# Down projection of a hybrid streaming layer: the next chunk's weight steps at fixed places over the chunk

## The chip, the cores and the metric

The kernel runs on one core of one Trainium2 chip. The metric is the time of one execution on the device in microseconds (us), the median of several runs; lower is better. Profiles show one execution, with the engines named PE (TensorE matmuls), PEld (TensorE weight loads), DVE (VectorE), ACT (ScalarE), POOL (GpSimd) and SP (SyncE, which issues DMAs).

## The reference, cut to what matters

One layer of a hybrid encoder is computed for 2048 prompt rows and 128 sample rows (17 tiles of 128 rows), in float32. The change touches only the last product of the feed-forward part:

```python
h = rmsnorm(x, norm_ffn_pre)
f = (jax.nn.silu(h @ w_gate) * (h @ w_up)) @ w_down     # w_down: 2816 x 1024
x = x + rmsnorm(f, norm_ffn_post)
```

## The kernel before, in words

**Stages.** The program runs the input projection and the two mixers, the output projection, gate and up, and last the down projection with the final norm. The down projection is the last stage; all before it stays as it is.

**How the down product is tiled.** The 22 blocks of 128 rows of `w_down` are cut into five chunks, `FCHUNKS`: four of 4 blocks and a last one of 6. Within a chunk two blocks make a 2 x 2 arrangement of quarters (b11, b12, b21, b22, each 128 x 512), and there are c = 2 such arrangements (q = 0, 1) in a chunk, c = 3 in the last. The product is done by a seven-product scheme in the manner of Strassen: step i = 0 to 6 multiplies one combination of activation rows by one combination of the quarters. Rows are taken in pairs of tiles: there are eight pairs (`pairs`, numbered 0 to 7 here) and one single tile. In each chunk the first two pairs run interleaved (the duo), then comes the single tile (four products), then pairs 2 to 7, one after the other; in the last chunk the single tile comes ahead of pair 7.

**Precision.** Every operand is split into a rounded part and the rest: a cast on ACT makes the first, a subtraction makes the second. Each product (`product`, L1567) is therefore 3 x c matmuls of 128 x 128 by 128 x 512, which read weights `dw` (or `sA` to `sD`, which serve as slots of the same ring) and activations `as`: 6 matmuls in a chunk with c = 2, 9 in the last.

**Activations.** `load_parts` (L1560) loads `ar` with SP's queue. `split` (L1551) casts on ACT (L1554) and subtracts (L1557): on DVE for i = 0 and 3 (in the last chunk i = 0 alone), on POOL for the rest. There are six `as` buffers (`NDA`), so the cast of a product waits until the product six before it has been done.

**Sums.** The result of a step goes from one of eight PSUM banks into `acc` in SBUF: by an addition on DVE (`acc_add`, L1534), in chunk 0 partly by a copy on ACT (L1614). A pair uses four banks; the bank of step 0 is used again by step 4, that of 1 by 5 and so on, so DVE has the time of three products to add a step's result before PE needs its bank. In the last chunk the finished rows are normed and stored as well (`finish`, L1577).

**The preparation of weights** is what the change moves. `down_chunk` (L1212) is a generator; each step of it either loads a q (two DMAs of `dr` from `w_dn` on SP's queue, L1220, into four `dr` buffers) or makes one part (i, q): for i = 1, 2, 3, 5 a subtraction of quarters on DVE (L1227 to L1233), then a cast on ACT (L1244), then the rest (L1246), every third on DVE and the others on POOL. A chunk with c = 2 has 2 loads and 14 parts. Parts go into a ring of `NDW` = 21 slots, so with a chunk's 14 parts in place there is room for seven of the next, and the other seven need slots that the current chunk's last pair gives free, two after each of its products. `prep_step(n)` runs n steps. It is called while a product lacks its weights (L1570), after each product of the last pair with n = c (L1666), and after pairs 2 to 6 with a share of `spare` = 9 (L1720). A step that finds the generator exhausted moves to the next chunk's generator and does nothing else.

**What sets the order.** A scheduler in the build writes the order of each engine's queue, and may set an instruction ahead of its place in the code where it finds its inputs ready. `tc.issue_after(ins)` holds the instructions of its block behind `ins` in the queue of the engine of `ins`. The queues of the engines then run in that order.

Of the kernel before, what the change touches and what calls it, by code (L numbers as in the profile page):

```python
# [9 lines left out]
F32 = mybir.dt.float32  # L10
# [3 lines left out]
ALU = mybir.AluOpType  # L14
# [40 lines left out]
NHX = 1  # L55
NST = 3
AHEAD = ("As", "Ts", "st", "st")
NWB = 12
# [5 lines left out]
NDW = 21  # L64
# [28 lines left out]
def kernel(  # L93
# [24 lines left out]
    V, A, G, T = nc.vector, nc.scalar, nc.gpsimd, nc.tensor  # L118
# [41 lines left out]
    with ExitStack() as ph:  # L160
# [801 lines left out]
        n = len(tiles)  # L962
        c = n * P
# [248 lines left out]
    def down_chunk(ch):  # L1212
# [36 lines left out]
        raw = {}  # L1249
        for lo in range(0, c, 2):  # L1250
            qs = range(lo, min(lo + 2, c))
            for q in qs:
                raw[q] = load(q)
                yield
            for i in range(7):
                for q in qs:
                    part(i, q)
                    yield

    def prep_step(n):  # L1260
        for _ in range(n):
            if dprep:
                try:
                    next(dprep[0])
                except StopIteration:
                    dprep.pop(0)
# [261 lines left out]
    with ExitStack() as ph:  # L1528
# [3 lines left out]

        def acc_add(dst, ps, eng=V):
            return eng.tensor_tensor(out=dst, in0=dst, in1=ps, op=ALU.add)  # L1534

# [15 lines left out]
        def split(v, e, first=False):  # L1551
            n = v.shape[-1]
            a = da.tile([P, 2, MC * P // 2], F32R, tag="as", name="as", bufs=NDA)
            ins = A.copy(a[:, 0, :n], v)  # L1554
            if first:
                cast[:] = [ins]
            e.tensor_tensor(out=a[:, 1, :n], in0=v, in1=a[:, 0, :n].bitcast(F32), op=ALU.subtract)  # L1557
            return a
# [57 lines left out]
        def down_pair(ch, u, last):  # L1616
# [19 lines left out]
            for i in (0, 1, 2, 3, 5, 4, 6) if final else range(7):  # L1636
# [23 lines left out]
                elif final and i > 3:  # L1660
                    half1(int(i == 6))
                    if i == 6:
                        factor1()
                        rest1()
                if last:
                    prep_step(c)  # L1666
                if duo:
# [120 lines left out]
```

## Time and profile before

| what | value |
|---|---|
| time before, median of 3 runs (lowest to highest) | 2452.97 us (2452.22 to 2453.81) |
| the profiled execution's own time | 2450.11 us |
| its span | 2448.2 us |
| DVE, ACT, POOL busy, share of the span | 66%, 43%, 23% |
| first matmul of the down projection | 1972.1 us |
| first matmul of chunks 1, 2, 3, 4 | 2057.4, 2140.87, 2223.79, 2308.06 us |
| end of its last matmul | 2436.9 us |

How to read the views that follow. Windows give, for each stretch of the span, the busy time of each engine and in brackets the instructions of which any part lies in it; overlapping matmuls count once in the busy time. The timeline gives start, length, engine, line, operation, and the number of like instructions in a row; what stands in square brackets is idle time of the engine ahead of it and what ended it. Groups give busy time, mean length in ns, and idle time before. A row of durations gives the shortest, median and longest in ns.

### The profile page before, as it was taken

Reading aid. Unit: us, or ns where it says so; the run is one execution under the profiler, and the core shown is the slowest. Engines: PE = TensorE matmul, PEld = TensorE weight load, DVE = VectorE, ACT = ScalarE, POOL = GpSimd, SP = SyncE. Lnnn points to the kernel's source line nnn. Section 1 sums busy time; section 2 is a strip of 40 time slices with the busy share of each in tenths; the row PEclk is TensorE's granted clock in tenths of the full one; section 3 lists DMA queues with packets and bytes.
Section 4 is the critical chain, followed back from the end, with each engine's and each line's share of the span. In section 5 each row is a group of like instructions: output and inputs, shape, how many; then the busy total and the mean of one; then the engine's idle time right before and its main releaser. Section 6 shows DMA issues by size and latency. Waiting matters only on the chain.

```text
span 2448.2 us, 39317 instructions
## 1 busy us (share of the span) xinstructions
PE 2424.2 (99%) x14360; PEld 2219.0 (91%) x14360; DVE 1620.6 (66%) x3070; ACT 1043.0 (43%) x2335; POOL 572.7 (23%) x664
## 2 busy tenths in 40 slices
PE   9999999999999999999999999999999999999997
PEld 7888889999989988899999999999999988887876
DVE  7875755746667356888888744456555565677698
ACT  6645546546444333444343422224333355333343
POOL 1101001001110000156655200000000056456664
PEclk9999999999999999999999999999999999999999
DMA  7774655766776657698877888888998744333475
GB/s 271 260 252 167 218 194 198 247 220 231 271 252 247 214 177 230 200 341 297 291 257 256 293 258 263 257 251 271 312 294 278 248 142 122 117 107 120 140 232 175
DMA packets 263465, 561.38 MB, mean 229 GB/s; under 512 B 25188, under 2 KB 144680, under 8 KB 245992
## 3 DMA queue, kind: packets, MB, share of 16 engines
q1 hardware_dynamic: 147024, 487.24, 59.1%
q10 hardware_dynamic: 116024, 70.58, 9.6%
q8 instruction: 113, 1.85, 0.3%
q0 software_dynamic: 224, 1.05, 0.1%
q14 instruction: 80, 0.66, 0.1%
HBM read 400.09 MB, written 158.70 MB: 228 GB/s over the span
## 4 chain that ended last, share of the span: by engine, by line
PE 87%; DVE 6%; issue 2%; DMA 2%; POOL 2%; ACT 1%; DVEq 0%; ACTq 0%; POOLq 0%; SPq 0%
PE fbank L1396 35%; PE dbank L317 26%; PE fbank L1574 11%; PE dbank L1161 4%; PE tbank L1161 4%; DVE xr L1599 1%; DVE acc L1534 1%; PE tbank L375 1%; POOL as L1557 1%; PE gbank L598 1%; PE gbank L605 1%; POOL dw L1246 1%; PE obank L777 1%; PE gbank L769 1%; PE ftbank L1190 1%
## 5 line engine op out<-in xcount | busy, mean ns | idle before, releaser
L1396 PE MATMUL fbank<-xh,fw 128*128 128x384 f32 (+1 forms) x3696 | 897.5, 326 | 0.7 <-ACT m L1428 0.6
L317 PE MATMUL dbank<-hi,w 128*128 128x384 f32 (+1 forms) x2240 | 655.5, 363 | 1.5 <-ACT w L296 0.8
L1396 PEld LDWEIGHTS fbank<-xh,fw 128*128 128x128 f32 x3696 | 650.8, 188 | 1.4 <-ACT m L1428 0.9
L1396 PE MATMUL fbank<-xl,fw 128*128 128x384 f32 (+1 forms) x1848 | 601.9, 326 | 0.0
L317 PEld LDWEIGHTS dbank<-hi,w 128*128 128x128 f32 x2240 | 412.5, 188 | 42.6 <-issue 3.6
L1574 PE MATMUL fbank<-dw,as 128*128 128x512 f32 x1782 | 420.8, 392 | 5.4 <-DVE acc L1534 2.9
L1574 PEld LDWEIGHTS fbank<-dw,as 128*128 128x128 f32 x1782 | 333.0, 188 | 85.1 <-POOL as L1557 3.5
L317 PE MATMUL dbank<-lo,w 128*128 128x384 f32 (+1 forms) x1120 | 399.6, 357 | 0.3 <-DVE lo L232 0.3
L1396 PEld LDWEIGHTS fbank<-xl,fw 128*128 128x128 f32 x1848 | 346.9, 188 | 0.0
L317 PEld LDWEIGHTS dbank<-lo,w 128*128 128x128 f32 x1120 | 210.7, 188 | 16.7 <-DVE lo L232 0.6
L1557 POOL TENSOR_TENSOR as<-ar,as 128x256 fp32r<-128x256 f32 (+1 forms) x202 | 183.5, 919 | 177.7 <-ACT as L1554 162.0
L1534 DVE TENSOR_TENSOR acc<-acc,fbank 128x512 f32<-128x512 f32 x246 | 164.0, 681 | 90.6 <-PE fbank L1574 77.2
L1246 POOL TENSOR_TENSOR dw<-dr,dw 128x512 fp32r<-128x512 f32 x48 | 70.1, 1472 | 504.2 <-ACT dw L1244 503.9
L1554 ACT CAST as<-ar 128x256 fp32r<-128x256 f32 (+1 forms) x287 | 116.5, 427 | 165.7 <-PE fbank L1574 123.0
L1371 ACT CAST fw<-rg 128x512 fp32r<-128x512 f32 x124 | 77.2, 622 | 233.8 <-PE fbank L1396 136.3
L321 DVE SCALAR_TENSOR_TENSOR acc<-R,vec,acc 128x512 f32<-128x512 f32 (+2 forms) x180 | 121.0, 673 | 28.6 <-ACT acc L358 22.7
L1444 DVE TENSOR_TENSOR c<-u,fbank 128x384 f32<-128x384 f32 (+1 forms) x66 | 34.9, 528 | 97.8 <-PE fbank L1396 97.8
L1440 DVE TENSOR_TENSOR m<-m,m 128x384 f32<-128x384 f32 (+1 forms) x44 | 23.1, 526 | 84.3 <-ACT m L1430 84.1
L1447 ACT ACTIVATE c<-c 128x384 f32<-128x384 f32 (+1 forms) x66 | 33.4, 506 | 97.5 <-DVE c L1446 97.5
L1372 POOL TENSOR_TENSOR fw<-rg,fw 128x512 fp32r<-128x512 f32 x44 | 64.1, 1458 | 45.4 <-ACT fw L1371 45.1
L350 POOL COPY hist<-R 128x3 f32<-128x3 f32 x60 | 20.0, 334 | 218.6 <-ACT R L326 169.3
L1442 ACT ACTIVATE m<-fbank 128x384 f32<-128x384 f32 (+1 forms) x66 | 31.2, 473 | 91.3 <-PE fbank L1396 74.4
(398 smaller groups left out, 3567.1 us busy)
## 6 DMA issues: line engine op xcount, KB each, us to landing
w<-wsplit SPq DMA_DIRECT2D x105, 1024.0 KB, 5.1
fw<-fsplit SPq DMA_DIRECT2D x188, 512.0 KB, 4.9
fsplit<-fw SPq DMA_DIRECT2D x94, 512.0 KB, 3.6
partd<-pt ACTq DMA_DIRECT2D x86, 384.0 KB, 5.8
rg<-in_w_gu SPq DMA_DIRECT2D x62, 512.0 KB, 4.3
wsplit<-w SPq DMA_DIRECT2D x28, 1024.0 KB, 5.2
wr<-in_w_in SPq DMA_DIRECT2D x34, 512.0 KB, 6.2
ar<-partd SPq DMA_DIRECT2D x43, 384.0 KB, 3.2
```

What stands on the lines that cost most here:

```text
L317: T.matmul(ps[:, :c], l[:, k, :], r[k][:, :c], start=(k == 0 and r is hi and l is wh), stop=(k == KD - 1 and l is wl))
L321: r = V.scalar_tensor_tensor(acc, raw(d), w[:, d:d + 1], acc, op0=ALU.mult, op1=ALU.add)
L1161: T.matmul(pss[n], m_[:, j, :], w_[k][:, n * 512:(n + 1) * 512], start=(k == 0 and ci == 0), stop=(k == KD - 1 and ci == 2))
L1246: e.tensor_tensor(out=w[1], in0=v, in1=w[0].bitcast(F32), op=ALU.subtract)
L1371: A.copy(w[:, 0], v)
L1372: e.tensor_tensor(out=w[:, 1], in0=v, in1=w[:, 0].bitcast(F32), op=ALU.subtract)
L1396: T.matmul(ps, w_[:, c], b_[k][:, :hw], start=(first and k == 0 and ci == 0), stop=(k == KH - 1 and ci == 2), skip_group_check=not first)
L1444: V.tensor_add(c21, u2, b3)
L1534: return eng.tensor_tensor(out=dst, in0=dst, in1=ps, op=ALU.add)
L1554: ins = A.copy(a[:, 0, :n], v)
L1557: e.tensor_tensor(out=a[:, 1, :n], in0=v, in1=a[:, 0, :n].bitcast(F32), op=ALU.subtract)
L1574: T.matmul(ps, a[:, x_, q * P:(q + 1) * P], w[y_], start=(start and q == 0 and ci == 0), stop=(q == c - 1 and ci == 2), skip_group_check=True)
```

## The change: where the steps of the preparation stand

Three things change; the arithmetic is the same.

First, the places. A table `STEPS` says for each chunk, pair and step i how many steps of the preparation follow that product. In chunks 0 to 2 the two loads follow step 0 of pair 2, seven single parts stand at (2,4), (3,1), (3,5), (4,2), (4,6), (5,3) and (6,0), that is four products apart, and six more follow steps 1 to 6 of the last pair; `LEFT` gives the remaining one to an early place in the next chunk's duo. For the last chunk, which has 3 loads and 21 parts, one load and the same seven places come first, then two loads at (6,3), eight parts in the last pair of chunk 3, and six parts in the duo of chunk 4. The calls after each pair and the `spare` are gone.

Second, each of these steps is held in the queues (`prep_behind`) behind the current product's instructions: the last cast on ACT, the last sum or split on DVE and the last split on POOL that were written by then (`mark_d`). SP's queue has no such mark.

Third, a generator that is exhausted no longer takes up a step (`while` with `break`), and the last chunk prepares its third q first, then q = 0 and 1.

```diff
+EARLY = {(2, 4): 1, (3, 1): 1, (3, 5): 1, (4, 2): 1, (4, 6): 1, (5, 3): 1, (6, 0): 1}
+STEPS = [{(2, 0): 2, **EARLY, **{(7, i): 1 for i in range(1, 7)}}] * 3
...
+LEFT = (0, 1, 1, 1, 6)
...
-        for lo in range(0, c, 2):
-            qs = range(lo, min(lo + 2, c))
+        for qs in ((0, 1),) if c == 2 else ((2,), (0, 1)):
...
     def prep_step(n):
         for _ in range(n):
-            if dprep:
+            while dprep:
                 try:
                     next(dprep[0])
+                    break
                 except StopIteration:
                     dprep.pop(0)
...
+        mark_d = {}
+
+        def acc_add(dst, ps):
+            mark_d["V"] = V.tensor_tensor(out=dst, in0=dst, in1=ps, op=ALU.add)
+            return mark_d["V"]
+
+        def prep_behind(n):
+            with ExitStack() as held:
+                for ins in mark_d.values():
+                    held.enter_context(tc.issue_after(ins.ins))
+                prep_step(n)
...
-            ins = A.copy(a[:, 0, :n], v)
+            ins = mark_d["A"] = A.copy(a[:, 0, :n], v)
...
-            e.tensor_tensor(out=a[:, 1, :n], in0=v, in1=a[:, 0, :n].bitcast(F32), op=ALU.subtract)
+            mark_d["V" if e is V else "G"] = e.tensor_tensor(out=a[:, 1, :n], in0=v, in1=a[:, 0, :n].bitcast(F32), op=ALU.subtract)
...
-                if last:
-                    prep_step(c)
+                prep_behind(STEPS[ch].get((pairs.index(u), i), 0))
...
-            spare = 0 if end else NDW - 7 * (len(chunk) // 2) + 2
             duo = [down_pair(ch, u, False) for u in pairs[:2]]
-            for i in (0, 1, 0, 0, 1, 1) + (0, 1) * 5 if not ch else (0, 1) * 8:
+            for n, i in enumerate((0, 1, 0, 0, 1, 1) + (0, 1) * 5 if not ch else (0, 1) * 8):
                 next(duo[i])
+                if 2 <= n < 2 + LEFT[ch]:
+                    prep_behind(1)
...
-                if k <= 6:
-                    prep_step(spare * (k - 1) // 5 - spare * (k - 2) // 5)
```

The queues show what this does. On POOL around the end of chunk 2, before: `as` (L1557) is the split of an activation, `dw`, `sA` and `sB` (L1246) the rest of a weight part.

```order
L1557 TENSOR_TENSOR as<-ar,as 128x256 x32
L1246 TENSOR_TENSOR dw<-dr,dw 128x512
L1557 TENSOR_TENSOR as<-ar,as 128x256 x2
L1246 TENSOR_TENSOR dw<-dr,dw 128x512 x4
L1557 TENSOR_TENSOR as<-ar,as 128x256 x4
L1246 TENSOR_TENSOR dw<-dr,dw 128x512 x3
L1557 TENSOR_TENSOR as<-ar,as 128x256
L1246 TENSOR_TENSOR dw<-dr,dw 128x512
L1557 TENSOR_TENSOR as<-ar,as 128x256 x33
```

The same place on POOL in the changed kernel, with the second half of chunk 2 ahead of it; the lines are now L1570 (split) and L1250 (weight part).

```order
L1570 TENSOR_TENSOR as<-ar,as 128x256 x11
L1250 TENSOR_TENSOR dw<-dr,dw 128x512
L1570 TENSOR_TENSOR as<-ar,as 128x256 x3
L1250 TENSOR_TENSOR sB<-dr,sA 128x512
L1570 TENSOR_TENSOR as<-ar,as 128x256 x5
L1250 TENSOR_TENSOR dw<-dr,dw 128x512
L1570 TENSOR_TENSOR as<-ar,as 128x256 x5
L1250 TENSOR_TENSOR dw<-dr,dw 128x512 x2
L1570 TENSOR_TENSOR as<-ar,as 128x256 x2
L1250 TENSOR_TENSOR dw<-dr,dw 128x512
L1570 TENSOR_TENSOR as<-ar,as 128x256 x2
L1250 TENSOR_TENSOR dw<-dr,dw 128x512 x2
```

Before, nine parts stood within seven splits and none in the 33 splits after them: the seven parts of the chunk after the next stood right behind the seven of the next. Now the early ones stand singly through the chunk, and around its end no more than two stand together.

On DVE at the end of chunk 3, before: `acc_1_21438` are the sums of the last pair, `acc_0_20787` and `acc_1_20808` those of the next chunk's duo, `dr<-dr` a subtraction of quarters, `dw` and `sD` weight parts, `as` an activation's split.

```order
L1534 TENSOR_TENSOR acc_1_21438<-acc_1_21438,fbank 128x512
L1246 TENSOR_TENSOR sD<-dr,sC 128x512
L1557 TENSOR_TENSOR as<-ar,as 128x384
L1534 TENSOR_TENSOR acc_1_21438<-acc_1_21438,fbank 128x512 x4
L1227 TENSOR_TENSOR dr<-dr 128x512
L1229 TENSOR_TENSOR dr<-dr 128x512
L1246 TENSOR_TENSOR dw<-dr,dw 128x512
L1231 TENSOR_TENSOR dr<-dr 128x512
L1246 TENSOR_TENSOR dw<-dr,dw 128x512
L1534 TENSOR_TENSOR acc_0_20787<-acc_0_20787,fbank 128x512
L1233 TENSOR_TENSOR dr<-dr 128x512
L1534 TENSOR_TENSOR acc_1_20808<-acc_1_20808,fbank 128x512
```

The same place on DVE in the changed kernel, where `acc_1_21442` is the last pair and L1231 to L1237 are the subtractions.

```order
L1540 TENSOR_TENSOR acc_1_21442<-acc_1_21442,fbank 128x512
L1231 TENSOR_TENSOR dr<-dr 128x512 x2
L1540 TENSOR_TENSOR acc_1_21442<-acc_1_21442,fbank 128x512
L1233 TENSOR_TENSOR dr<-dr 128x512
L1250 TENSOR_TENSOR dw<-dr,dw 128x512
L1540 TENSOR_TENSOR acc_1_21442<-acc_1_21442,fbank 128x512
L1233 TENSOR_TENSOR dr<-dr 128x512
L1235 TENSOR_TENSOR dr<-dr 128x512
L1540 TENSOR_TENSOR acc_1_21442<-acc_1_21442,fbank 128x512
L1235 TENSOR_TENSOR dr<-dr 128x512
L1540 TENSOR_TENSOR acc_0_20787<-acc_0_20787,fbank 128x512
L1250 TENSOR_TENSOR sD<-dr,sC 128x512
```

Here six subtractions have come in among the last four sums of chunk 3, two of each kind: these belong to the eight parts that the last pair now prepares. Before, the sums of the last pair were done ahead of the subtractions.

On SP the order of the loads is nearly as it was: of the four `dr` loads at the end of a chunk one or two have moved behind an `ar` load and the load of the single tile, and the two loads of the last chunk's third q, which stood among the first loads of chunk 4, have gone into the chunk before.

More of the change, by code (lines that the diff above doesn't have):

```diff
@@ L56 @@
 NST = 3
+EARLY = {(2, 4): 1, (3, 1): 1, (3, 5): 1, (4, 2): 1, (4, 6): 1, (5, 3): 1, (6, 0): 1}
+STEPS = [{(2, 0): 2, **EARLY, **{(7, i): 1 for i in range(1, 7)}}] * 3
+STEPS += [{(2, 0): 1, **EARLY, (6, 3): 2, (7, 1): 1, (7, 2): 1, (7, 3): 2, (7, 4): 1, (7, 5): 2, (7, 6): 1}, {}]
+LEFT = (0, 1, 1, 1, 6)
 AHEAD = ("As", "Ts", "st", "st")
@@ L1531 @@
         MC = max(len(c) for c in FCHUNKS)
-        def acc_add(dst, ps, eng=V):
-            return eng.tensor_tensor(out=dst, in0=dst, in1=ps, op=ALU.add)
+        mark_d = {}
[7 more added lines that the diff above has]
+                prep_step(n)
         def rows(u):
```

## The prediction

> **What bounds the kernel now.** First the page: the span, PE's share, and PE's lines in the chain that ended last.
>
> ```profile
> span 2448.2 us, 39317 instructions
> PE 2424.2 (99%) x14360; PEld 2219.0 (91%) x14360; DVE 1620.6 (66%) x3070; ACT 1043.0 (43%) x2335; POOL 572.7 (23%) x664
> PE fbank L1396 35%; PE dbank L317 26%; PE fbank L1574 11%; PE dbank L1161 4%; PE tbank L1161 4%; DVE xr L1599 1%; DVE acc L1534 1%; PE tbank L375 1%; POOL as L1557 1%; PE gbank L598 1%; PE gbank L605 1%; POOL dw L1246 1%; PE obank L777 1%; PE gbank L769 1%; PE ftbank L1190 1%
> ```
>
> PE is at work all the time, and the change leaves its matmuls as they are. What can be won is the time in which a matmul of the down projection (L1574) starts late. The busy share hides that, since matmuls overlap, so the second view is windows: one for each chunk 0 to 3, then the last chunk up to 2375 and its rest. A chunk of c = 2 has 60 products, 360 matmuls.
>
> ```profile
> 1972.10:2057.40 85.30, 83.51 (x362) 67.30 (x361) 49.95 (x70) 50.65 (x116) 48.99 (x49) 1.00 0.44 132
> 2057.40:2140.87 83.47, 83.18 (x362) 67.38 (x360) 58.24 (x89) 30.33 (x74) 46.26 (x51) 1.00 0.40 123
> 2140.87:2223.79 82.92, 82.74 (x362) 67.25 (x360) 58.12 (x89) 28.68 (x70) 46.45 (x50) 1.00 0.38 113
> 2223.79:2308.06 84.27, 83.56 (x361) 67.24 (x360) 57.85 (x90) 30.10 (x73) 45.94 (x50) 1.00 0.40 124
> 2308.06:2375.00 66.94, 66.18 (x289) 53.75 (x287) 58.23 (x88) 27.40 (x65) 48.16 (x42) 1.00 0.65 214
> 2375.00:2436.90 61.90, 59.89 (x252) 46.75 (x252) 57.85 (x95) 22.19 (x59) 29.80 (x27) 1.00 0.66 198
> ```
>
> Third, windows over a quiet stretch in the middle of each of chunks 0 to 3, and the length of one matmul.
>
> ```profile
> 2008.00:2047.00 39.00, 39.00 (x171) 31.82 (x170) 12.20 (x22) 18.83 (x44) 14.76 (x20) 1.00 0.38 109
> 2082.00:2130.00 48.00, 48.00 (x211) 39.29 (x210) 27.06 (x45) 13.45 (x34) 18.25 (x25) 1.00 0.35 101
> 2160.00:2214.00 54.00, 54.00 (x240) 44.69 (x239) 31.82 (x55) 15.64 (x41) 19.70 (x27) 1.00 0.40 113
> 2245.00:2298.00 53.00, 53.00 (x232) 43.13 (x232) 30.33 (x52) 14.68 (x38) 19.75 (x27) 1.00 0.37 110
> L1574 PE MATMUL fbank<-dw,as x1782: 387/389/505, 1972.1 to 2436.5; 128*128 128x512 f32 x198
> ```
>
> A matmul counts if any part of it lies in the window, so the pitch is (length + 0.389) / count: 0.2304, 0.2293, 0.2266 and 0.2301 us. Times 360 that is 82.9, 82.6, 81.6 and 82.8 us, and the chunks took 2.4, 0.9, 1.3 and 1.4 us more: about 6.0 us of late matmuls. (One matmul more or less in a count moves a chunk by 0.35 to 0.5 us.) Fourth, the timeline of PE says where.
>
> ```profile
> 1976.92 0.40 PE L1574 MATMUL fbank<-sB,as 128*128 128x512 f32 x1
> 1978.27 1.20 PE L1574 MATMUL fbank<-dw,as 128*128 128x512 f32 x4 [0.96 <-DVE as L1557]
> ...
> 2006.73 5.37 PE L1574 MATMUL fbank<-dw,as 128*128 128x512 f32 x22 [0.84 <-DVE acc L1534]
> ...
> 2078.87 1.66 PE L1574 MATMUL fbank<-dw,as 128*128 128x512 f32 x6 [0.18 <-DVE acc L1534]
> ...
> 2156.36 71.76 PE L1574 MATMUL fbank<-dw,as 128*128 128x512 f32 x312 [0.15 <-POOL as L1557]
> ...
> 2238.40 6.81 PE L1574 MATMUL fbank<-dw,as 128*128 128x512 f32 x26 [0.68 <-POOL as L1557]
> ```
>
> The first is at the start of chunk 0 (1978.27 - 1976.92 - 0.23 = 1.1 us); the others lie 35, 21, 15 and 15 us into chunks 0 to 3. PE waits there for a sum on DVE or a split on POOL, never for a weight. What keeps DVE and POOL, the groups of 2059 to 2080 show (DVE first, then POOL).
>
> ```profile
> L1534 DVE TENSOR_TENSOR acc<-acc,fbank 128x512 f32<-128x512 f32 x13 | 8.6, 676 | 1.7 <-PE fbank L1574 1.7
> L1557 DVE TENSOR_TENSOR as<-ar,as 128x256 fp32r<-128x256 f32 x5 | 4.0, 800 | 1.6 <-ACT as L1554 1.6
> L1229 DVE TENSOR_TENSOR dr<-dr 128x512 f32<-128x512 f32 x2 | 2.4, 1212 | 0.0
> L1231 DVE TENSOR_TENSOR dr<-dr 128x512 f32<-128x512 f32 x2 | 2.0, 981 | 0.0
> L1246 DVE TENSOR_TENSOR dw<-dr,dw 128x512 fp32r<-128x512 f32 x2 | 1.9, 955 | 0.0
> L1227 DVE TENSOR_TENSOR dr<-dr 128x512 f32<-128x512 f32 x2 | 1.9, 952 | 0.0
> L1233 DVE TENSOR_TENSOR dr<-dr 128x512 f32<-128x512 f32 x1 | 0.7, 679 | 0.0
> ...
> L1557 POOL TENSOR_TENSOR as<-ar,as 128x256 fp32r<-128x256 f32 x11 | 10.9, 1007 | 0.0
> L1246 POOL TENSOR_TENSOR dw<-dr,dw 128x512 fp32r<-128x512 f32 x5 | 7.2, 1448 | 1.8 <-ACT dw L1244 1.6
> ```
>
> DVE is busy for 21.5 of 21 us (a little reaches over the edges), 8.9 of them for weights, and POOL for 18.1, of them 7.2. In the quiet stretch of that chunk DVE had 27.06 of 48 (56%) and POOL 18.25 (38%). So PE is late where two sevens of parts stand together, and only there.
>
> **The change part by part.** *The early seven parts leave the chunk's beginning.* With them go the 8.9 and 7.2 us from a stretch that DVE could not fill. I take all lateness behind those bursts as gone: 2.4 - 1.1 = 1.3 us in chunk 0, 0.9, 1.3 and 1.4 in chunks 1 to 3, together 4.9 us. What is late next is nothing in this stretch: without the burst DVE has 12.6 of 21 us there. The bounds are the counting error of about 0.4 us for each chunk, say 4.0 to 5.8 in all. The start of chunk 0 has its order unchanged and keeps its 1.1.
>
> *The seven parts among the middle pairs.* In a stretch like the quiet 48 us they bring DVE to (27.06 + 8.9) / 48 = 75% and POOL to 53%. The queues are strict, so what counts is a single place.
>
> ```profile
> L1227 DVE TENSOR_TENSOR dr<-dr x11: 680/1210/1775, 1863.1 to 2313.0; 128x512 f32<-128x512 f32 x11
> L1244 ACT CAST dw<-dr x69: 602/620/632, 1837.7 to 2321.6; 128x512 fp32r<-128x512 f32 x69
> L1246 POOL TENSOR_TENSOR dw<-dr,dw x48: 1282/1466/1800, 1838.4 to 2323.1; 128x512 fp32r<-128x512 f32 x48
> ```
>
> On DVE a sum is put back by one subtraction, 0.7 to 1.8 us. It has three products (18 x 0.229 = 4.1 us) less its own 0.68, so 3.4 us: hidden. On ACT a part's cast stands behind that of an activation made six products ahead, and costs 0.62 us plus a wait for its subtraction, about a product (1.4 us); on POOL the rest takes at most 1.8. Together 3.8 us of the lead of five products, 6.9 us: hidden. I take 0; the lower bound is 0 too, as PE gains nothing from spare time elsewhere, and the upper bound is 0.5 us, a couple of stalls like those of 0.15 and 0.18.
>
> *The end of a chunk.* Seven parts still stand around the last pair; on POOL no more than two or three in a row, 3 x 1.5 = 4.4 us, again below the lead of 6.9. Take 0, at most 0.5 for all chunks.
>
> *Chunks 3 to 4.* Here it gets tighter. Eight parts stand in the last pair of chunk 3, six behind; six subtractions (0.7 to 1.2 each by the groups) and a rest lie among four sums: 4 x 0.68 + 6 x 0.7 + 0.7 = 7.6, up to 11 us, in about 5.5 us of PE. DVE enters chunk 4 with 2 to 5.5 us of debt, and POOL has eight rests (8 x 1.45 = 11.6 us) among seven splits of 128 x 384. But a product lasts 9 x 0.229 = 2.06 us there, and in the duo a bank comes round after seven products. I take 0.4 us, bounds 0 and 1.5.
>
> *SP.* The four weight loads in a chunk stand a little later in SP's queue, behind them an `ar` load and the single tile's.
>
> ```profile
> 2055.27 3.46 SPq L1220 DMA_DIRECT2D dr<-in_w_dn x4
> ...
> 2065.86 0.33 SPq L1564 DMA_DIRECT2D ar<-lastd  x1
> ```
>
> That load went out at 2065.86 for a product that PE reaches 14 x 1.37 us after 2057.4, at 2076.6: 10.7 us of cover. Cost 0. The other edits (the exhausted generator, the third q first) only decide places.
>
> *Sum.* The profiled execution: 2450.11 - 4.9 + 0.4 = 2445.6 us, its span 2443.7. It lay 2.9 us below the median of the runs; with the same difference the median goes from 2452.97 to 2448.5.
>
> **The rivals.** *The bubbles come from the ring.* If the 21 slots were what PE waits for, moved steps would only move the wait, and the time would stay at 2453 (2451 to 2454). Perfetto Trace Analysis in the Trainium skill (section Optimization Strategy) speaks for this: the same gap repeating on the engine that should be saturated can mean too few buffers for the next tile. By that rule the sum would be 0 instead of -4.9. The rows speak against it: PE waited for L1534 and L1557, and a weight part at L1246 ended none of the waits above.
>
> *A locked port.* L1227 takes 0.68 us or up to 1.78, the longer while POOL works. If each early subtraction met a split, and a rest on DVE met another, a sum would be 2 x 1.78 = 3.6 us late, over its 3.4, by 0.2; with the part's own wait for ACT half a microsecond. With four subtractions in each of four sevens, 16 x 0.15 takes half the gain: 2450.9. SBUF in the Trainium skill (section SBUF: two separate sides) has the harder form: VectorE with two SBUF inputs and GpSimd share a port pair, and the loser blocks for the whole instruction. By it a subtraction could take 0.68 + 1.47 = 2.15 us, an estimate; the trace's longest, 1.78, is below that. Against this rival: nearly all early subtractions and rests have a sum between them.
>
> *Slower: the cast blocks ACT.* A part's cast waits for its subtraction, which stands behind a sum and so behind PE; if PE runs closer to ACT than six products, all splits wait at each of 28 early places. This decides from 4.9 / 28 = 0.18 us for each place. At 0.46 us (a stop of 0.18 and the slow restart around it, as in the 0.9 us of chunk 1 for two) it is 28 x 0.46 = 12.9: 2453 + 8 = 2461. Against it, the idle of ACT in the quiet windows (13.45 busy of 48).
>
> *More than counted.* If chunk 4's DVE, busy 57.85 of 61.90 us, is also relieved, 2 us more go: 2446. But its order from the first norm on is the same.
>
> **How the numbers follow.** A measurement of this kernel can tell about 0.2%, 4.9 us, from no change: the line is at 2448.06, right beside the forecast. Forecast (2446.6 to 2450.2) 0.66, of it 0.32 below the line; ring 0.12; port 0.09; slower 0.06; more than counted 0.07. Faster 0.32 + 0.07 = 0.39; same 0.34 + 0.12 + 0.09 = 0.55; slower 0.06. The range reaches from 2445.5 (the larger gain) to 2452.5 (most of the ring's case) and leaves out the slow one and a little of both ends.
>
> **What would show it.** Right: chunks 1 to 3 each take 82 to 83 us from first matmul to first matmul, chunk 0 about 84, chunk 4 and the tail as before; PE's waits for L1534 and L1557 near 2007, 2079, 2156 and 2238 are gone; DVE shows no stretch of 20 us that is full before 2308. Wrong: chunks as long as before with the stops elsewhere (the ring); many small stops between pairs 2 and 6 (port or ACT); a stop of more than 1.5 us within 25 us of chunk 4's start.

## The result, and the profile after

Measured side by side, the changed kernel took 2447.39 us (median of 14 runs, 2445.83 to 2449.44), the kernel before 2452.29 us (14 runs, 2450.37 to 2454.19): a ratio of 0.9981, 95% interval 0.9974 to 0.9988, so 4.9 us less. The profiled execution of the changed kernel took 2445.83 us. First two lines of its page and the windows of the five chunks, chunk 4 in two parts (start:end and length, then PE, PEld, DVE, ACT, POOL busy, clock, DMA share, GB/s).

```profile
span 2444.1 us, 39297 instructions
PE 2421.2 (99%) x14360; PEld 2219.9 (91%) x14360; DVE 1619.4 (66%) x3070; ACT 1045.0 (43%) x2335; POOL 568.9 (23%) x664
```

```profile
1971.73:2055.63 83.90, 82.95 (x362) 67.45 (x361) 47.32 (x69) 50.22 (x115) 44.21 (x47) 1.00 0.42 133
2055.63:2138.14 82.51, 82.51 (x362) 67.52 (x360) 57.72 (x89) 29.27 (x72) 45.05 (x52) 1.00 0.39 119
2138.14:2219.80 81.66, 81.66 (x362) 67.56 (x360) 58.27 (x91) 29.71 (x73) 44.22 (x50) 1.00 0.39 120
2219.80:2302.53 82.73, 82.73 (x361) 67.50 (x360) 55.78 (x89) 31.22 (x74) 46.20 (x52) 1.00 0.43 140
2302.53:2375.00 72.47, 70.57 (x305) 56.73 (x304) 67.72 (x97) 31.97 (x76) 54.43 (x44) 1.00 0.61 188
2375.00:2432.72 57.72, 55.88 (x237) 43.72 (x235) 53.89 (x89) 18.95 (x49) 27.54 (x25) 1.00 0.66 209
```

In chunks 1 to 3 PE's busy time is now the whole length, 82.51 of 82.51 us and so on: no gap at all. The busy sums of DVE and POOL are nearly as before (1619.4 us for 1620.6, 568.9 for 572.7), so the same work lies elsewhere. Against before, chunks 0 to 3 lost 1.40, 0.96, 1.26 and 1.54 us, 5.16 together. Chunk 4 took 72.47 + 57.72 = 130.19 us against 128.85, 1.34 more. The stages ahead ended 0.37 us earlier (1971.73 for 1972.10), which the change does not touch, and the tail is the same. -5.16 + 1.34 - 0.37 = -4.19: the span went from 2448.2 to 2444.1.

What PE waited for in chunks 0 to 3 (us in total, times, longest), in the kernel before and then in the changed one.

```profile
PE fbank L1574 <- DVE acc L1534: 1.0, 2, 0.8
PE fbank L1574 <- DVE as L1557: 1.0, 1, 1.0
PE fbank L1574 <- POOL as L1557: 0.8, 2, 0.7
```

```profile
PE fbank L1587 <- DVE as L1570: 0.9, 1, 0.9
```

What is left is the stop at the start of chunk 0. The view counts only PE's full idleness. A matmul lasts 0.39 us and the next starts 0.23 us behind it, so one can start up to 0.16 us late with no idle time, and the second one behind a stop starts 0.34 us after the first. By the starts in the trace, the matmuls of chunks 0 to 3 that came more than 0.24 us behind the one ahead were late by 6.3 us in total before and 1.2 us after, which is nearly all of the 5.16 us. The stretch at the start of chunk 1 shows why, before and after.

```profile
2059.00:2080.00 21.00, 20.71 (x89) 16.26 (x88) 19.35 (x27) 9.19 (x23) 17.18 (x16) 1.00 0.41 131
```

```profile
2059.00:2080.00 21.00, 21.00 (x93) 17.16 (x92) 12.32 (x21) 6.77 (x18) 11.83 (x14) 1.00 0.55 175
```

DVE fell from 19.35 to 12.32 us of 21 and POOL from 17.18 to 11.83. (The prediction added up the groups of this stretch to 21.5 us on DVE; by the windows, which count a moment once and nothing outside the stretch, it was 19.35.) Last, three of PE's stops in chunk 4 of the changed kernel, and behind them the first stop of that chunk before (start, length, what it ran, in brackets the idle time ahead and what ended it).

```profile
2323.94 12.22 PE L1587 MATMUL fbank<-dw,as 128*128 128x512 f32 x52 [0.18 <-POOL as L1570]
...
2354.97 10.60 PE L1587 MATMUL fbank<-dw,as 128*128 128x512 f32 x45 [0.33 <-DVE acc L1540]
...
2370.91 5.18 PE L1587 MATMUL fbank<-dw,as 128*128 128x512 f32 x20 [1.26 <-DVE acc L1540]
```

```profile
2375.07 3.34 PE L1574 MATMUL fbank<-dw,as 128*128 128x512 f32 x12 [0.83 <-DVE acc L1534]
```

The first two are new. One is a split on POOL, at the end of the duo, where the late weight parts stand; the other is a sum in the stretch of the norms, in a window where DVE has 67.72 of 72.47 us. The third is the old stop at the norms, 68.4 us into the chunk where it was 67.0, and 0.43 us longer.

### The profile page after: what moved, and what is told of

Read it like the earlier page. It is cut to its first block, busy times and chain, and to the rows that moved or that the text cites. A ratio compares the mean times of both kernels' runs of the same rounds, so it can differ in the third digit from the quotient of the medians.

```text
span 2444.1 us, 39297 instructions
## 1 busy us (share of the span) xinstructions
PE 2421.2 (99%) x14360; PEld 2219.9 (91%) x14360; DVE 1619.4 (66%) x3070; ACT 1045.0 (43%) x2335; POOL 568.9 (23%) x664
## 4 chain that ended last, share of the span: by engine, by line
PE 90%; DVE 5%; DMA 2%; issue 1%; POOL 1%; ACT 1%; DVEq 0%; SPq 0%; ACTq 0%; POOLq 0%
PE fbank L1400 35%; PE dbank L321 26%; PE fbank L1587 13%; PE dbank L1165 4%; PE tbank L1165 4%; DVE xr L1612 1%; PE tbank L379 1%; DVE acc L1540 1%; PE gbank L602 1%; PE gbank L609 1%; PE obank L781 1%; PE gbank L773 1%; PE gbank L795 1%; PE ftbank L1194 1%; PE obank L803 1%
## 5 line engine op out<-in xcount | busy, mean ns | idle before, releaser
L1570 POOL TENSOR_TENSOR as<-ar,as 128x256 fp32r<-128x256 f32 (+1 forms) x202 | 182.7, 915 | 170.4 <-ACT as L1567 158.5
L1250 POOL TENSOR_TENSOR dw<-dr,dw 128x512 fp32r<-128x512 f32 x48 | 67.7, 1419 | 512.8 <-ACT dw L1248 510.1
```

Of the source, the lines that this page charges most:

```text
L1250: e.tensor_tensor(out=w[1], in0=v, in1=w[0].bitcast(F32), op=ALU.subtract)
L1570: mark_d["V" if e is V else "G"] = e.tensor_tensor(out=a[:, 1, :n], in0=v, in1=a[:, 0, :n].bitcast(F32), op=ALU.subtract)
```

## The experiments

Each of the twelve kernels was timed in five rounds beside the kernel before. All start from the changed kernel unless the diff says otherwise. The table has each chunk from its first matmul to the next chunk's, chunk 4 to the end of its last matmul, and the tail behind it, all worked out from starts and ends in the profiled execution, in us; the last column is the ratio to the kernel before with its 95% interval.

| kernel | 0 | 1 | 2 | 3 | 4 | tail | ratio |
|---|---|---|---|---|---|---|---|
| before | 85.30 | 83.47 | 82.92 | 84.27 | 128.85 | 11.3 | |
| changed | 83.90 | 82.51 | 81.66 | 82.73 | 130.19 | 11.3 | 0.9981 (0.9974 to 0.9988) |
| e1 not held | 85.02 | 83.63 | 82.93 | 82.74 | 131.13 | 11.3 | 0.9999 (0.9990 to 1.0008) |
| e2 seven at one place | 83.89 | 82.53 | 82.07 | 82.73 | 130.77 | 11.6 | 0.9983 (0.9974 to 0.9992) |
| e3 old end | 83.90 | 82.51 | 81.66 | 82.68 | 129.12 | 11.3 | 0.9975 (0.9965 to 0.9984) |
| e4 last chunk's split on POOL | 83.90 | 82.51 | 81.66 | 82.73 | 128.68 | 11.3 | 0.9976 (0.9966 to 0.9986) |
| e5 one more op | 83.89 | 82.51 | 81.66 | 82.73 | 130.76 | 11.3 | 0.9980 (0.9971 to 0.9989) |
| e6 three more ops | 84.32 | 82.50 | 82.52 | 85.14 | 133.05 | 11.6 | 1.0007 (0.9998 to 1.0016) |
| e7 = e3 and e4 | 83.90 | 82.51 | 81.66 | 82.68 | 130.67 | 11.3 | 0.9983 (0.9974 to 0.9992) |
| e8 = e7, differences on POOL | 83.91 | 82.51 | 81.66 | 82.68 | 133.45 | 12.7 | 0.9997 (0.9988 to 1.0006) |
| e9 fourteen in a row, held | 83.89 | 82.51 | 82.93 | 82.73 | 131.05 | 11.5 | 0.9989 (0.9980 to 0.9997) |
| e10 = e4, norms spread | 83.90 | 82.51 | 81.66 | 82.73 | 128.19 | 16.0 | 0.9987 (0.9978 to 0.9996) |
| e11 = e10, three steps | 83.91 | 82.51 | 81.66 | 82.74 | 127.18 | 13.7 | 0.9980 (0.9971 to 0.9989) |
| e12 block on DVE | 83.89 | 88.02 | 86.57 | 90.99 | 130.14 | 11.3 | 1.0053 (1.0040 to 1.0067) |

Where nothing touches a chunk its length repeats to 0.01 or 0.02 us from kernel to kernel, so the chunks tell more than the times of whole runs, whose spread is 2 to 5 us. Chunk 4 is less steady: e2 and e5 change only the steps of chunks 0 to 3, and it takes 0.6 us more in them.

### What removed the stops: e1, e2 and e9

**e1: the places, but not the holding.**

```diff
         def prep_behind(n):
-            with ExitStack() as held:
-                for ins in mark_d.values():
-                    held.enter_context(tc.issue_after(ins.ins))
-                prep_step(n)
+            prep_step(n)
```

> The changed kernel with its places and its counts, but the steps are written without being held behind the current cast, split and sum. In the queues the early seven parts then stand right behind the fourteen before them again, as in the kernel before. If it is the clump of parts on DVE and POOL that made PE late, and the holding that dissolves it: the chunks take about 85.3, 83.5, 82.9 and 84.3 us again and the time is that of the kernel before, 2452.3 (2451 to 2453.5). If the places in the table are what counts: 2447.4, no stop of over 0.3 us at 15 to 35 us into chunks 0 to 3.

Measured: 2450.41 us beside 2451.38 for the kernel before, ratio 0.9999. PE's timeline in this kernel (L1585 is the matmul, L1568 the split), of chunks 0 to 2 and then of chunk 4, with the lines between left out:

```profile
2006.94 5.37 PE L1585 MATMUL fbank<-dw,as 128*128 128x512 f32 x22 [0.81 <-DVE acc L1540]
2077.19 0.50 PE L1585 MATMUL fbank<-sC,as 128*128 128x512 f32 x1 [0.38 <-POOL as L1568]
2156.73 71.77 PE L1585 MATMUL fbank<-dw,as 128*128 128x512 f32 x312 [0.15 <-POOL as L1568]
2322.37 2.34 PE L1585 MATMUL fbank<-dw,as 128*128 128x512 f32 x9 [0.36 <-POOL as L1568]
2325.85 4.39 PE L1585 MATMUL fbank<-dw,as 128*128 128x512 f32 x18 [1.13 <-ACT as L1565]
```

The stops of chunks 0 to 2 are back within 2 us of their old places. So the table of places alone does nothing in these chunks: a step that is not held is set forward by the scheduler to where its inputs are ready, right behind the parts ahead of it. In chunk 1 the subtractions of quarters on DVE start from 2062.1 to 2076.5 us in e1, and from 2061.9 to 2076.7 in the kernel before. It also ends the theory of the ring: the ring is the same in e1 and in the changed kernel, and PE stops in the one and not in the other. One point missed: the stop of chunk 3 did not come back (82.74), but two more came in chunk 4 (131.13). The last chunk's new order, third q first, is kept here, and it makes the clump of chunk 3 lighter: from 2226 to 2241 DVE runs four subtractions in e1 and seven in the kernel before. I did not separate the two, so what removed the stop of chunk 3 stays open.

**e2: the early seven held, all at one place.**

```diff
-EARLY = {(2, 4): 1, (3, 1): 1, (3, 5): 1, (4, 2): 1, (4, 6): 1, (5, 3): 1, (6, 0): 1}
+EARLY = {(3, 1): 7}
```

> The changed kernel with the early seven parts of each chunk all behind step 1 of pair 3, held as before: a clump of seven, without the other seven ahead of it. If a clump is what costs: five subtractions and two rests of about 0.95 us are 6.7 us on DVE against 3.4 us of cover, PE stops there in chunks 0 to 3, by 0.3 to 1 us each, 2448.6 to 2451.4. If the ring's slots were the limit and the change had only given them more time: as the changed kernel, 2447.4, because the parts are still made 25 products ahead of their use. If seven are no clump and only fourteen together are: 2447.4 too, but with DVE full for about 7 us and no stop.

Measured: 2446.90 us, ratio 0.9983. In chunks 0 to 3 PE waited, in total:

```profile
PE fbank L1587 <- DVE as L1570: 1.0, 1, 1.0
```

That is the old stop at the start of chunk 0. Seven parts at one place cost nothing where they stand. Chunk 2 takes 0.4 us more, in late starts near 2151, 17 us ahead of the first of these parts. My price for a clump, 6.7 us on DVE against 3.4 us of cover, was wrong: the parts do not stand as one block, since the scheduler sets sums between them.

**e9: fourteen in a row, each held.** In chunks 1 to 3 the early seven follow the late seven, one behind each product of the duo.

```diff
-STEPS = [{(2, 0): 2, **EARLY, **{(7, i): 1 for i in range(1, 7)}}] * 3
-STEPS += [{(2, 0): 1, **EARLY, (6, 3): 2,
+STEPS = [{(2, 0): 2, **EARLY, **{(7, i): 1 for i in range(1, 7)}}]
+STEPS += [{(7, i): 1 for i in range(1, 7)}] * 2
+STEPS += [{(6, 3): 2,
...
-LEFT = (0, 1, 1, 1, 6)
+LEFT = (0, 10, 10, 9, 6)
```

> The changed kernel, but in chunks 1 to 3 the early seven parts (and the loads ahead of them) follow the late seven at once, one behind each product of the duo, every one held: fourteen in a row as in the kernel before, with the holding kept. If the row of fourteen is the cause whatever its order in the queue: a product's 1.37 us on DVE would have a sum of 0.68, 0.2 of splits and 0.9 of a part, 0.4 us too much, fourteen times, 5.6 us less the 3.4 of cover: PE stops for up to 2 us about 10 to 25 us into chunks 1 to 3, 2448.5 to 2452. If what costs is that several parts stand in the queue between two sums, and one at a time is harmless: as the changed kernel, 2447.4 (2446.5 to 2448).

Measured: 2449.08 us, ratio 0.9989. Windows of chunks 1 to 3 and of a stretch early in chunk 2, then the like stretch of the kernel before:

```profile
2056.24:2138.74 82.50, 82.50 (x361) 67.56 (x360) 57.42 (x88) 28.62 (x71) 46.83 (x51) 1.00 0.39 118
2138.74:2221.67 82.93, 82.72 (x362) 67.21 (x360) 59.20 (x92) 29.78 (x74) 46.43 (x51) 1.00 0.38 118
2221.67:2304.40 82.73, 82.73 (x361) 67.56 (x360) 57.79 (x87) 30.00 (x72) 46.30 (x50) 1.00 0.43 140
2143.00:2164.00 21.00, 20.90 (x90) 16.30 (x89) 18.16 (x25) 8.04 (x19) 17.51 (x15) 1.00 0.48 163
```

```profile
2145.00:2166.00 21.00, 20.82 (x89) 16.04 (x88) 19.93 (x29) 7.57 (x19) 15.17 (x14) 1.00 0.34 93
```

Between the two theories. DVE and POOL are nearly as full there as before (18.16 and 17.51 of 21 us, against 19.93 and 15.17), yet only chunk 2 loses anything, 1.27 us; before, chunks 1 to 3 lost 0.96, 1.26 and 1.54. The holding, which lets each part stand behind a sum, so saves the stop of chunk 1 by itself; that of chunk 2 needs the spreading as well. For chunk 3 this run shows nothing, since its stop is gone in e1 too, which holds nothing. The other 0.9 us, in chunk 4, comes with a stop of 1.3 us on a POOL split that e2 and e5 show too.

### How much cover there is: e5, e6 and e12

**e5 and e6: more work on DVE at the early places**, here with one; e6 has three.

```diff
+            for _ in range(heavy[0]):
+                V.tensor_tensor(out=v, in0=v, in1=v, op=ALU.max)
             n = len(dring)
...
+                heavy[0] = 1 if (pairs.index(u), i) in EARLY else 0
                 prep_behind(STEPS[ch].get((pairs.index(u), i), 0))
+                heavy[0] = 0
```

> The changed kernel with one more DVE instruction ahead of each of the 28 early parts: the maximum of the quarter with itself, written in place, of the same shape and with two SBUF operands as a subtraction of quarters has; the values stay the same. If the cover for a sum is 3.4 us as the prediction has it: a place then holds two such instructions, at most three, of 0.7 to 1.2 us, 1.4 to 3.4 us in all, and the time stays at 2447.4 (up to 2448.2). If a cast that waits on ACT, or the port, takes the cover first: 0.18 us or more for each place, 28 x 0.18 = 5 us, 2452 or more.

> The same with three more DVE instructions ahead of each early part. In the 5.5 us from place to place DVE has four sums (2.7 us), 1.1 splits of 0.8 us, and of a part 0.7 subtractions and 0.3 rests, 1.0 us: 4.6 us. Three more of 0.7 to 1.0 make it 6.7 to 7.6, 1.2 to 2.1 us too much at each place; seven places are 8.4 to 14.7 us, less a cover of 3.4 us: 5 to 11 us for each of chunks 0 to 3, 2467 to 2492, with PE waiting for sums. If the cover were much larger (a sum that may be late by a whole pair): under 2455.

Measured: e5 2446.63 us beside 2451.66, ratio 0.9980, chunks 0 to 3 unchanged to 0.01 us, as expected. e6 2453.73 us, ratio 1.0007: far below the 2467 to 2492 expected. Windows of chunk 1 in e6 and in the changed kernel, and DVE's timeline in e6, where L1241 is the added instruction, L1543 a sum and L1232 a subtraction:

```profile
2080.00:2138.00 58.00, 58.00 (x255) 47.46 (x254) 52.76 (x84) 22.20 (x52) 36.76 (x35) 1.00 0.32 96
```

```profile
2080.00:2138.00 58.00, 58.00 (x255) 47.44 (x254) 41.99 (x64) 21.51 (x51) 29.70 (x35) 1.00 0.32 96
```

```profile
2100.88 0.68 DVE L1543 TENSOR_TENSOR acc<-acc,fbank 128x512 f32<-128x512 f32 x1
2101.48 0.68 DVE L1241 TENSOR_TENSOR dr<-dr 128x512 f32<-128x512 f32 x1
2102.08 0.67 DVE L1543 TENSOR_TENSOR acc<-acc,fbank 128x512 f32<-128x512 f32 x1
2102.68 0.68 DVE L1241 TENSOR_TENSOR dr<-dr 128x512 f32<-128x512 f32 x1
2103.28 0.68 DVE L1543 TENSOR_TENSOR acc<-acc,fbank 128x512 f32<-128x512 f32 x1
```

DVE is busy 52.76 of 58 us and PE still loses nothing in chunk 1. The added instructions alternate with sums, and the steps slip back over the rest of the chunk; the work is not due until the chunk's end. It shows there, and behind it: chunk 3 gets 2.4 us longer, 1.5 of them in its last 16 us, and chunk 4 2.9, where PE waits 1.1 us for a weight part on DVE at 2317.15. Chunks 0 and 2 lose 0.4 and 0.9 us. My arithmetic took a step for a block at its place; a hold sets only the earliest place.

**e12: a block that cannot be cut.**

```diff
+        few = dn.tile([P, 64], F32, name="few")
...
+                if pairs.index(u) in (3, 4, 5) and i == {1: 0, 2: 3, 3: 0}.get(ch):
+                    with tc.issue_after(mark_d["V"].ins):
+                        V.tensor_reduce(out=few, in_=acc[pairs[0]][:, 0, :64].unsqueeze(2).broadcast_to([P, 64, 88]), op=ALU.max, axis=AX.X)
```

> The changed kernel with nine long DVE instructions more, each one reduction of 128 x 5632 elements (64 values read 88 times) into a scratch tile, about 6 us by the 0.60 us that a reduction of 128 x 384 takes in the profile: in chunks 1 and 3 behind the sum of step 0 of pairs 3, 4 and 5, in chunk 2 behind that of step 3 of the same pairs. Unlike the three instructions of e6 it cannot be cut by sums. If every sum has a cover of 3.4 us, as the prediction has it: the sum behind the block is late by 0.7 (the sum before) + 6 + 0.7 - 1.4 - 4.1 = 1.9 us at all nine places: 17 us, 2464 (2459 to 2469), in chunks 1, 2 and 3 alike. If only the sums of steps 0 to 2 have it, because the banks of steps 3 to 6 come round a whole pair later: 5 to 6 us in chunks 1 and 3 each, nothing in chunk 2, 2458 (2455 to 2460). If the cover is far larger everywhere, as e6 could be read: 2447.4 to 2449.

Measured: 2465.61 us beside 2452.56, ratio 1.0053. The block's row (shortest, median, longest in ns), and all stops over 1 us of PE in chunks 1 to 3, with the lines between left out:

```profile
L1681 DVE TENSOR_REDUCE few<-acc x9: 6005/6006/6014, 2092.9 to 2291.6; 128x64 f32<-128x5632 f32 x9
```

```profile
2111.75 3.28 PE L1588 MATMUL fbank<-dw,as 128*128 128x512 f32 x7 [2.40 <-DVE as L1571]
2122.30 3.69 PE L1588 MATMUL fbank<-dw,as 128*128 128x512 f32 x15 [1.06 <-DVE acc L1541]
2219.05 17.26 PE L1588 MATMUL fbank<-dw,as 128*128 128x512 f32 x74 [2.60 <-DVE acc L1541]
2287.78 7.15 PE L1588 MATMUL fbank<-dw,as 128*128 128x512 f32 x30 [1.63 <-DVE as L1571]
2298.32 5.04 PE L1588 MATMUL fbank<-dw,as 128*128 128x512 f32 x14 [3.39 <-DVE acc L1541]
```

Chunks 1 to 3 take 5.5, 4.9 and 8.3 us more. The theory that spared steps 3 to 6 falls, as chunk 2 pays too. The sum, 18.7 us, is near the 17 us of a cover of 3.4 us at every place, but that is luck. The places are not alike: the first block of each chunk costs nothing, later ones 1.0 to 3.4 us of idle PE. Two of the stops are followed by slow stretches that cost 1.5 and 1.6 us (last section), and a stop of 0.90 us, at 2244.03, comes ahead of chunk 3's first block. The queue of PE explains why the places differ. Here is its order in the changed kernel in the middle of chunk 1 (bank, weights, activations): `fbank_21744` takes step 6 of one pair, `fbank_21833` step 0 of the next, `fbank_21834` its step 1.

```
L1587 MATMUL fbank_21833<-dw_21066,as_21837 128x512
L1587 MATMUL fbank_21833<-dw_21120,as_21837 128x512 x2
L1587 MATMUL fbank_21744<-sC_21536,as_21817 128x512
L1587 MATMUL fbank_21744<-sD_21537,as_21817 128x512
L1587 MATMUL fbank_21744<-sC_21536,as_21817 128x512
L1587 MATMUL fbank_21744<-dw_21560,as_21817 128x512 x3
L1587 MATMUL fbank_21833<-dw_21120,as_21837 128x512
L1587 MATMUL fbank_21834<-dw_21164,as_21847 128x512 x3
```

The next pair's step 0 is woven into this pair's last steps: PE's order is the scheduler's too. Read with the starts in the trace, the gap from a bank's step to its reuse is in most pairs 4.1 us for step 0 (the 3.4 of the prediction, with a sum of 0.68), 4.6 for step 1 and 5.2 to 5.5 for step 2. Where the scheduler knew of the block it set more of the next pair ahead: behind the first block of chunk 1, sixteen matmuls of the next pair come ahead of the step that needs the late sum, where two stand in the changed kernel.

### Chunk 4: e3, e4 and what was built on them

**e3: the last chunk's later parts prepared as before.**

```diff
-        for qs in ((0, 1),) if c == 2 else ((2,), (0, 1)):
+        for lo in range(0, c, 2):
+            qs = range(lo, min(lo + 2, c))
...
-STEPS += [{(2, 0): 1, **EARLY, (6, 3): 2, (7, 1): 1, (7, 2): 1, (7, 3): 2, (7, 4): 1, (7, 5): 2, (7, 6): 1}, {}]
-LEFT = (0, 1, 1, 1, 6)
+STEPS += [{(2, 0): 2, **EARLY}, {}]
+LEFT = (0, 1, 1, 1, 0)
...
                 prep_behind(STEPS[ch].get((pairs.index(u), i), 0))
+                if ch == 3 and last:
+                    prep_step(c)
```

> The changed kernel in chunks 0 to 2 and in the early seven of chunk 3, but the rest of the last chunk's weights is prepared as in the kernel before: q = 0 and 1 first, two steps after each product of chunk 3's last pair, nothing held there and none set into the duo. If chunk 4 became 1.3 us longer because of the eight parts among the last sums of chunk 3 and the six in the duo, it takes 128.9 us again and the time is 2446.1 (2445.5 to 2446.7). If the 1.3 us comes from what chunk 4 has itself, or from the slots that its parts got: no difference, 2447.4. If the old end brings back the clump: slower by up to 1 us, in the last 10 us of chunk 3 or the first 20 of chunk 4.

Measured: 2445.13 us beside 2451.38, ratio 0.9975. Chunk 4 takes 129.12 us, 1.07 less than in the changed kernel, and its first stop is now that of the norms:

```profile
2370.59 3.34 PE L1588 MATMUL fbank<-dw,as 128*128 128x512 f32 x12 [1.25 <-DVE acc L1541]
```

The stops at 2323.94 and 2354.97 are gone. So most of the 1.34 us was the price of the new end: eight parts among the last sums, six in the duo, the third q first. This edit undoes them together and does not say which. The stop of the norms stays as long as in the changed kernel (1.25 us, 0.83 before), so its growth is not the new end's; what made it stays open.

**e4: step 0's split of the last chunk on POOL.**

```diff
-                e = V if i in ((0,) if end else (0, 3)) or
+                e = V if i in (() if end else (0, 3)) or
```

> The changed kernel, with the split of step 0 in the last chunk on POOL instead of DVE (in all nine of its units but the single tile, which keeps DVE). If DVE is the bound of the last chunk, whose 57 of 62 us are full: 8 x 0.55 = 4.4 us leave DVE, and of the 5.5 us in which PE stops there 1 to 2.5 go: 2445.0 to 2446.4. If POOL's longer split (1.0 to 1.2 us) or the slower DVE beside it eats that: 2447.4 or up to 1 us slower.

Measured: 2445.36 us beside 2451.38, ratio 0.9976; chunk 4 takes 128.68 us, 1.51 less. DVE's busy time in the chunk falls from 121.6 to 119.1 us, 2.5 and not the 4.4 expected, and the stop of the norms to 0.82 us.

**e7 and e8: both, and more of DVE's work on POOL.** e7 has the edits of e3 and e4; e8 also this one:

```diff
             if end and not last:
-                V.tensor_sub(a2, a4, a2)
-                V.tensor_sub(a3, a4, a3)
+                G.tensor_tensor(out=a2, in0=a4, in1=a2, op=ALU.subtract)
+                G.tensor_tensor(out=a3, in0=a4, in1=a3, op=ALU.subtract)
```

> The two edits that each made it faster, together: the last chunk's later parts prepared as in the kernel before, and step 0's split of the last chunk on POOL. If both take the same excess of DVE in the last chunk: no better than either, 2445.2. If they take different stops (the places at 20 and 50 us into chunk 4, and the norm's at 68 to 125 us): 2443.4 (2442.8 to 2444.2).

> As e7, and the two differences of sums at the end of each finished pair of the last chunk (a4 - a2 and a4 - a3) on POOL instead of DVE: 14 instructions of 0.7 to 1.5 us leave DVE. If DVE's load is what stops PE in the last chunk: of the 3 us or so of stops that are left, half go, 2442.0 (2441 to 2443). If the stops that are left come from one long chain in the norm, or POOL's 1.45 us and the port cost as much: as e7 or up to 2 us slower.

Measured: e7 2447.67 us, ratio 0.9983; e8 2450.62, ratio 0.9997, both beside 2451.66. Both miss what was expected of them. The intervals of e7 overlap those of e3 and e4, but by chunk 4 each takes longer than what it builds on (130.67 us against 129.12 and 128.68, then 133.45). In e7 a slow stretch of 1.6 us behind one stop (last section) is as much as its 1.55 us over e3. Windows from 2320 to 2360 of e7, then of e8:

```profile
2320.00:2340.00 20.00, 20.00 (x89) 16.40 (x88) 15.51 (x24) 10.52 (x27) 17.39 (x16) 1.00 0.54 169
2340.00:2360.00 20.00, 19.06 (x84) 15.36 (x83) 19.75 (x30) 6.83 (x19) 11.42 (x11) 1.00 0.86 281
```

```profile
2320.00:2340.00 20.00, 20.00 (x89) 16.37 (x88) 9.60 (x15) 8.56 (x20) 19.03 (x18) 1.00 0.53 165
2340.00:2360.00 20.00, 16.72 (x74) 13.37 (x72) 20.00 (x28) 7.11 (x21) 17.06 (x15) 0.98 0.64 197
```

In e8 DVE idles 10 us of the first window, while the differences stand in POOL's full queue (19.03 of 20), and then has many norms at once, ahead of sums: one sum reached PE 6 us late. The load of DVE in the chunk fell and PE lost more. By this run what counts is what stands ahead of a sum at the moment it is due.

**e10 and e11: the norms of the finished pairs at fixed places as well**, two steps behind each product in e10 and three in e11, held like the weight steps, on top of e4.

```diff
             if end and not last:
-                V.tensor_sub(a2, a4, a2)
-                V.tensor_sub(a3, a4, a3)
-                r1, r2 = rows(u)
-                finish_all((a1, a3), [(0, r1)])
-                finish_all((a2, a4), [(0, r2)])
+                norms.append(finish_pair(a1, a2, a3, a4, u))
...
+                if end and i < 4:
+                    norm_behind(99 if final and i == 3 else RATE)
+                elif end and not final:
+                    norm_behind(RATE)
```

> As e4 (step 0's split of the last chunk on POOL), and the norms of the finished pairs of the last chunk are cut in steps too and set at two steps behind each product, held behind the current cast, split and sum; before, the norms of the duo's two pairs fell due together. If PE's stops in the last chunk come from norms standing ahead of sums in DVE's queue: the 4.3 us of stops of e4 go to about 1, 2442 (2441 to 2443.5). If the norms only get late and meet at the end: the tail behind the last matmul grows from 11.3 us by 1 to 4 and eats it, 2444 to 2447.

> As e10 with three steps behind each product, so that no norm is left over for the end. If the steps left over at the end of e10 cost there: up to 1 us faster than e10. If three steps, some 2.4 us of DVE, are too much beside a sum in a product of 2.06 us: PE stops in pairs 2 to 4 again, as e4, 2445.

Measured: 2449.27 us, ratio 0.9987, and 2446.91, ratio 0.9980, both beside 2452.07. Chunk 4 falls to 128.19 and 127.18 us, the shortest seen, but the tail grows from 11.3 to 16.0 and 13.7. So e10 came out above the 2444 to 2447 of the second case, and e11 2.4 us below e10 where at most 1 was expected. Windows behind the last matmul, in e10 and in the changed kernel:

```profile
2432.45:2448.40 15.95, 0.00 (x0) 0.00 (x0) 9.03 (x19) 2.35 (x8) 2.02 (x3) 0.62 0.54 164
```

```profile
2432.72:2444.00 11.28, 0.00 (x0) 0.00 (x0) 6.63 (x13) 2.17 (x6) 1.10 (x2) 0.61 0.36 134
```

DVE has 19 instructions there instead of 13: the norms came late and met at the end, and what PE gained was given back. e3 and e4 stay the fastest kernels here; against the changed kernel their intervals overlap, and the 1.1 and 1.5 us are read from the chunks.

## Why the prediction was right, point by point

**What bounds the kernel.** Right. The stops 15 to 35 us into chunks 0 to 3 were all that the change could take, and it took them; e1 brings those of chunks 0 to 2 back with the same places and the same ring. The signs came as named: the four waits are gone, and no 20 us of chunks 0 to 3 have DVE busy for more than 17.8 us, where before it reached 19.9. Two signs did not fit: chunk 4 is not as before, and chunk 2 took 81.66 us and not 82 to 83, though the prediction's own sum for it (82.92 - 1.3) gives 81.6.

**The early seven leave the chunk's beginning, -4.9 us.** Measured -5.16 in chunks 0 to 3 (expected 1.3, 0.9, 1.3 and 1.4; measured 1.40, 0.96, 1.26 and 1.54). What was left out is that the places do it only with the holding: e1 has the places and no gain in chunks 0 to 2, e2 holds all seven at one single place and has nearly all of the gain. In chunk 3 the lighter clump of the new order may have been enough by itself, which e1 suggests.

**The middle pairs, 0.** Right in size: PE has no gap in chunks 1 to 3, and e5 adds an instruction at each place and loses nothing in chunks 0 to 3. The reasoning was wrong in its picture: no step stands as a block at its place (e6), and three products of cover hold for step 0's bank alone, because PE's queue weaves the pairs. The blocks of e12 give the order of size of the cover and no more than that.

**The end of a chunk and SP, 0.** Right: no wait in chunks 1 to 3 is left.

**Chunks 3 to 4, +0.4 (0 to 1.5).** Within its bounds and mis-sized: +1.34, of which e3 takes away 1.07. I priced DVE's debt in the duo; what came was a split on POOL at 2323.94 and a late sum 31 us further on, among the norms, where DVE has little slack to pay back a debt. What e3 leaves is the longer stop of the norms, whose cause stays open. There the argument that chunk 4's order is the same from the first norm on gave no safety.

**Sum.** 2445.6 for the profiled execution, 2445.83 measured, and so near because errors cancel: 0.26 more gained and 0.94 more lost than reckoned, 0.37 from earlier stages, and 0.09 less outside the span. To be within 0.22 us is luck, too, as the down projection starts anywhere from 1970.89 (e4) to 1974.35 us (e8) in kernels whose code is the same up to there. The median, forecast at 4.5 us below that of before, came 4.9 below it.

**The rivals.** The ring: out by e1. Perfetto Trace Analysis in the Trainium skill (section Optimization Strategy) says that gaps that repeat like these can mean too few buffers; here they went with the same 21 slots, and those of chunks 0 to 2 came back with them. The locked port and the cast that blocks ACT: PE shows no stop between pairs 2 and 6, and e5 nearly doubles the early DVE instructions without cost in chunks 0 to 3, so neither decides. More than counted: the opposite, chunk 4 got longer.

## What to carry to other kernels

Where a scheduler may set work forward, a table of places can do nothing until each step is held behind something (chunks 0 to 2 of e1); and a hold sets the earliest place only, so a step's cost is not that of a block. Side work was free while the helpers of the bound engine still reached each due result in time, however full they were (52.76 of 58 us here); in a stage where they are full to the end, the same work, or its delay, came back as stops or in the tail. Look at the stage's own length by its chunks, which repeat to 0.02 us where nothing touches them, when whole runs spread by 2 to 5 us.

## What the runs showed of the hardware that was not expected

**A stop of little more than 2 us can halve PE's clock.** In e7 PE was late by 2.16 us at 2371.54. Every second window of 1 us from there on (the clock stands behind the five busy times):

```profile
2371.00:2372.00 1.00, 0.46 (x2) 0.45 (x3) 0.75 (x2) 0.91 (x3) 0.00 (x0) 1.00 0.56 217
2373.00:2374.00 1.00, 1.00 (x4) 0.81 (x3) 1.00 (x3) 1.00 (x5) 0.96 (x2) 0.50 0.39 86
2375.00:2376.00 1.00, 1.00 (x4) 0.72 (x3) 1.00 (x2) 0.47 (x1) 1.00 (x1) 0.51 1.00 406
2377.00:2378.00 1.00, 0.71 (x4) 0.25 (x2) 0.95 (x3) 0.00 (x0) 0.50 (x1) 1.00 0.58 211
```

The granted clock is 0.50 for some 3.4 us, and eight matmuls start 427 ns apart instead of 229: 1.6 us on top of the stop. It came behind stops of 2.57 and 3.55 us in e12 and 6.1 us in e8 too, and not behind one of 2.21 us in e11 and one of 2.76 in e12 (all by the starts of the matmuls). TensorE: Matmul & The Clock Gate in the Trainium skill (Part 1: The HAM clock gate) has a free-running window of about 3.4 us, and the clock halved after one idle window; the length of the slow stretch agrees, but the stops of 2.16 and 2.57 us are shorter than such a window, and were enough. Why they were, and the 2.76 us were not, is not shown.

**The same matmul has several pitches.** In the changed kernel's chunk 2 nearly all matmuls start 226 or 227 ns apart, in chunks 0, 1 and 3 some products run at 231 to 236, by the starts in the trace, and so again in the other kernels with the same slots. This, and no wait, is why chunk 2 takes 81.66 us and chunk 1 82.51 with PE busy throughout. The cause was not tried.
